# The first layer's modulated input takes its slots half by half

## The chip, the cores and the metric

The kernel runs on one core of a Trainium2 chip. The metric is the device time of one execution in microseconds (us). The core has five engines with an instruction queue each: TensorE (PE in the rows; its weight loads are PEld), VectorE (DVE), ScalarE (ACT), GpSimd (POOL) and SyncE (SP), which here only issues transfers. Each engine works its queue in order; a wait at the head of a queue holds everything behind it.

## The reference, cut to what matters

Two layers of a backbone. Each modulates a normalized input, multiplies it by one wide matrix, runs four branches on slices of the product, and merges them. 128 context tokens and 512 latent tokens go through the same weights with different conditioning vectors (`c_ctx` and `c`).

```python
def trunk_layer(x, cond, p, latent, k_ctx, v_ctx):
    mod = jax.nn.silu(cond) @ p['w_ada'] + p['b_ada']
    shift, scale, gate = jnp.split(mod, 3, axis=-1)
    h = rms_norm(x, p['norm_g']) * (1.0 + scale) + shift
    y, k, v = parallel_mixer(h, p, latent, k_ctx, v_ctx)
    return x + gate * y, k, v
```

`h` of the first layer is what the change is about. Inside `parallel_mixer`, `u = h @ p['w_in']` feeds, among others, a long convolution (Hyena) whose filters are made by a small network, brought into the frequency domain, and multiplied with the transformed input.

## The kernel before

**Numbers and tiles.** All 640 tokens (128 context, 512 latent) are processed together; a projection makes 128 channels at a time, in two pieces of 320 tokens. A product in 32 bits is made of three: the weight and the activation are each split into a rounded part and a rest (`whi`, `wlo`, and `Act.hi`, `Act.lo`), and `proj` adds hi*hi, hi*lo and lo*hi. One piece is 16 matmuls with `whi` and 8 with `wlo`, 24 in all. `split(hi, lo, src)` casts on ScalarE and subtracts on VectorE: that subtraction reads two tiles in SBUF.

**Slots.** SBUF is mostly 13 large slots (`NSLOT`), handed out by `slot()` in the order in which they came free. In the first microseconds they hold the conditioning rows (`s_cond`), the small parameters (`s_prm`), the input of the filter network (`s_hid`), the residual stream in two halves of the channels (`xs[0]`, `xs[1]`: sl_120 and sl_121 in the rows), two filter slots, the tables, and four of the eight chunks of the first layer's modulation matrix `w_ada` (sl_175, sl_178, sl_181, sl_184); the other four chunks lie in weight buffers.

**The start.** `ada_first` takes the chunks in the order 0 4 1 5 2 6 3 7. A chunk is 8 matmuls against the conditioning columns `cs` into an `ax` buffer, a copy to a `k` tile on ScalarE, two transposes of that tile (the `ax<-ident,k` rows) and small additions into `mod` on VectorE. Chunks 0 and 4 give the modulation of channel blocks 0 and 1, chunks 1 and 5 of blocks 2 and 3, and so on: `ev_mod[0][k // 2]`.

**The modulated input.** `modulated_first` (line 758) scales x by the inverse norm, and then, for each half `h` and channel block `c`, transposes the block's tokens to PSUM, applies scale and shift into a `t` tile (latent tokens on ScalarE, context tokens on VectorE), and splits it into `a.h(k)` and `a.l(k)`. Blocks 0 to 3 lie in the first slot of `a.hi` and of `a.lo`, blocks 4 to 7 in the second. The first projection waits for each block by `a.ev[j][k]` (in `proj`). Before the change the function is started by `layers()` only when `new_act(2)` has got all four slots, the two of `hi` first:

```python
            if l == 0:
                a = yield from new_act(2)
                a.ev = [[Event(lm) for _ in range(8)] for _ in range(2)]
                lm.spawn(modulated_first(a, xs, ssq), PN)
```

**What sets the order.** The kernel is written as cooperating threads, run by the planner `Loom` while the program is made: it keeps a modelled time of each engine, and at each `yield` takes the ready thread of the highest priority. PE's order is exactly the order in which the planner let the threads issue; the other engines' orders follow from it and from priorities. So a change in when one thread can go on re-sorts the rest of the program behind it. Two other threads matter here. `Hyena.filters(q)` makes the filters of four channel blocks c, each for two orders q: matmuls `ax<-k,hd`, a product on VectorE, squares on ScalarE, sums on GpSimd, and `spectrum` (the `sc<-sl,sl` and `ax<-sl,sl` rows). `Hyena.run` convolves; when it is done with block 0 it frees slots, and the filter inputs of block 3 are fetched into one of them.

Of the kernel before, what the change touches and what calls it, by code (L numbers as in the profile page):

```python
# [10 lines left out]
F32R = mybir.dt.float32r  # L11
# [220 lines left out]
def hybrid_flow_backbone(ctx: ExitStack, tc: tile.TileContext, i, o):  # L232
# [49 lines left out]
    def slot(dt=F32):  # L282
        yield lambda: 0.0 if free else INF
        return Slot(dt)
# [28 lines left out]
    def split(hi, lo, src, scale=None):  # L313
        if scale is None:
            act.copy(hi, src)
            dve.tensor_tensor(out=lo, in0=src, in1=r32(hi), op=ALU.subtract)
        else:
            act.activation(out=hi, in_=src, func=AF.Copy, scale=scale)
            dve.scalar_tensor_tensor(out=lo, in0=src, scalar=scale, in1=r32(hi),
                                     op0=ALU.mult, op1=ALU.subtract)  # L320
# [53 lines left out]
    def slots(n, dt=F32):  # L374
        r = []
        for _ in range(n):
            r.append((yield from slot(dt)))
        return r

    def new_act(n):  # L380
        hi = yield from slots(n, F32R)
        lo = yield from slots(n, F32R)
        return Act(hi, lo)
# [365 lines left out]
    def rms(ssq):  # L749
        n = ssq.shape[1]  # L750
        v = sm.tile([P, 5], F32, tag="rmsv", name=nm("rmsv"))[:, 0:n]
        rs = sm.tile([P, 5], F32, tag="rmsr", name=nm("rmsr"))[:, 0:n]
        dve.tensor_reduce(out=v, in_=ssq, axis=AX.X, op=ALU.add)
        dve.tensor_scalar(out=v, in0=v, scalar1=1.0 / D, scalar2=EPS, op0=ALU.mult, op1=ALU.add)
        power(rs, v, n)
        return rs

    def modulated_first(a, xs, ssq):

        rs = rms(ssq)  # L760
        for h in range(2):
            xv = xs[h].v(0, 5, 512)
            for t in range(5):
                dve.tensor_scalar(out=xv[:, t, :], in0=xv[:, t, :], scalar1=rs[:, t:t + 1], scalar2=None,
                                  op0=ALU.mult)
        for h in range(2):
            xv = xs[h].v(0, 5, 512)
            yield lm.sync()
            pp = yield from ax.get()
            for c in range(4):  # L770
                pe.transpose(pp[:, 128 * c:128 * c + 128], xv[:, 0, 128 * c:128 * c + 128], ident)
            for c in range(4):
                k = 4 * h + c
                yield ev_mod[0][k // 2]
                ps = yield from mm.get()
                for t in range(4):
                    pe.transpose(ps[:, 128 * t:128 * t + 128], xv[:, 1 + t, 128 * c:128 * c + 128], ident)
                hf = yield from tr.get(T)
                A, S = mods[0][:, 1, k, :], mods[0][:, 0, k, :]
                act.activation(out=hf[:, 128:640], in_=ps, func=AF.Identity, scale=A[:, 1:2], bias=S[:, 1:2])  # L780
                dve.tensor_scalar(out=hf[:, 0:128], in0=pp[:, 128 * c:128 * c + 128], scalar1=A[:, 0:1],
                                  scalar2=S[:, 0:1], op0=ALU.mult, op1=ALU.add)
                mm.put()
                split(a.h(k), a.l(k), hf)
                tr.put()
                for j in range(2):
                    a.ev[j][k].set()
            ax.put()
            xs[h].free()
# [1100 lines left out]
    def layers():  # L1890
# [3 lines left out]
        for l in range(DEPTH):  # L1894
            hy = hys[l]
            if l == 0:
                a = yield from new_act(2)
                a.ev = [[Event(lm) for _ in range(8)] for _ in range(2)]
                lm.spawn(modulated_first(a, xs, ssq), PN)
            hT[0] = a  # L1900
# [77 lines left out]
            if l + 1 < DEPTH:  # L1978
# [3 lines left out]
                a = yield from new_act(2)  # L1982
# [79 lines left out]
    lm.spawn(ada_first(chunks), 3)  # L2062
    lm.spawn(first_sums(*x_first), 4)
    lm.spawn(layers(), 6)
    with tc.manual_schedule(engines={mybir.EngineType.PE}):
        lm.run()
# [94 lines left out]
```

## Time and profile before

| | us |
|---|---|
| median of 3 runs | 2257.85 |
| lowest, highest | 2257.24, 2259.43 |
| the profiled execution | 2260.89 |
| its span (first to last instruction) | 2258.9 |

| engine | busy us | share of the span |
|---|---|---|
| PE | 2191.6 | 97% |
| DVE | 1320.8 | 58% |
| ACT | 1191.5 | 53% |
| POOL | 593.5 | 26% |

The profile is one execution. The busy share says that TensorE is the bound; what it doesn't say is how much of a stretch TensorE ran at its lower clock, which the column of the granted clock shows (1.00 is 2.4 GHz, 0.50 is 1.2 GHz, and a stretch between is a mixture).

### The profile page before, as it was taken

To read this page: it belongs to the slowest core of one execution; us is meant where nothing else is said; L and a number is where in the kernel's file an instruction comes from. 1 tells how busy PE (TensorE), PEld (TensorE's weight loads), DVE (VectorE), ACT (ScalarE), POOL (GpSimd) and SP (SyncE) were. 2 spreads that over 40 slices of the span, in tenths; PEclk is the share of its full clock that TensorE was granted. 3 is DMA by queue.
4 is the path that set the end of the run, shared out by engine and by line. 5 is a ranking of instruction groups with operands and counts; after the bars stand their busy time and mean duration, and the time that the engine had idled before them with its cause. 6 is when DMAs were issued, how large, how long until landed. Compare 5 with 4: busy or idle time off the path is not lost. (4 is left out here: it accounts for less than half of the span.)

```text
span 2258.9 us, 39947 instructions
## 1 busy us (share of the span) xinstructions
PE 2191.6 (97%) x15951; PEld 2141.9 (95%) x15951; DVE 1320.8 (58%) x2736; ACT 1191.5 (53%) x2179; POOL 593.5 (26%) x456
## 2 busy tenths in 40 slices
PE   5998999999999999999999999899999999999999
PEld 3898999999999999999998999899999999999998
DVE  5676686466669965344224768746655898512222
ACT  5554456576664336444446453667766533544441
POOL 2644321111111222564221332111111122222221
PEclk9999999999999999999999999999999999999999
DMA  9476776454658888787899765575555788698985
GB/s 278 113 155 134 157 152 115 91 111 81 106 108 163 150 141 174 156 166 162 150 224 206 140 115 126 130 144 102 93 105 108 144 150 150 121 159 147 172 175 132
DMA packets 510534, 322.31 MB, mean 143 GB/s; under 512 B 13016, under 2 KB 499608, under 8 KB 510093
## 3 DMA queue, kind: packets, MB, share of 16 engines
q0 software_dynamic: 223856, 122.96, 42.9%
q1 hardware_dynamic: 285780, 196.68, 28.8%
q8 instruction: 125, 2.05, 0.4%
q14 instruction: 60, 0.49, 0.1%
q10 hardware_dynamic: 713, 0.14, 0.0%
HBM read 302.26 MB, written 17.47 MB: 142 GB/s over the span
## 5 line engine op out<-in xcount | busy, mean ns | idle before, releaser
L192 PE MATMUL mm<-sl,whi 128*128 128x320 f32 x6304 | 1061.9, 313 | 9.5 <-ACT whi L177 2.9
L192 PEld LDWEIGHTS mm<-sl,whi 128*128 128x128 f32 x6304 | 951.1, 189 | 17.9 <-DVE sl L177 4.7
L192 PE MATMUL mm<-sl,wlo 128*128 128x320 f32 x3152 | 552.2, 311 | 0.5 <-DMA wlo<-in_w_in_dram 0.5
L346 POOL DMA_DIRECT2D wlo<-in_w_in_dram x173 | 264.5, 1529 | 891.6 <-ACT wlo L177 648.1
L192 PEld LDWEIGHTS mm<-sl,wlo 128*128 128x128 f32 x3152 | 482.4, 188 | 1.7 <-DMA wlo<-in_w_in_dram 0.7
L177 ACT CAST whi<-raw 128x1024 fp32r<-128x1024 f32 (+2 forms) x272 | 255.3, 939 | 400.9 <-PE mm L192 379.6
L177 ACT ACTIVATE wlo<-whi 128x1024 fp32r<-128x1024 f32 (+2 forms) x269 | 254.9, 948 | 29.5 <-PE mm L192 26.1
L177 DVE SCALAR_TENSOR_TENSOR t<-t,mm 128x320 f32<-128x320 f32 x192 | 93.0, 485 | 288.2 <-PE mm L192 239.7
L192 PE MATMUL mm<-whi,sl 128*128 128x256 f32 x1600 | 227.3, 285 | 1.9 <-ACT u L177 1.5
L177 DVE SCALAR_TENSOR_TENSOR sc<-sl,prm,sc 128x640 f32<-128x640 f32 (+14 forms) x232 | 207.4, 894 | 9.5 <-ACT sc L177 4.9
L192 PEld LDWEIGHTS mm<-whi,sl 128*128 128x128 f32 x1600 | 204.6, 189 | 4.2 <-ACT u L177 2.2
L192 PE MATMUL sc<-sl,sl 128*128 128x128 f32 (+1 forms) x1344 | 202.4, 292 | 2.7 <-DVE u L177 1.6
L177 DVE TENSOR_TENSOR h<-ax,h 128x512 fp32r<-128x512 f32 (+1 forms) x200 | 120.8, 604 | 121.8 <-ACT h L177 120.5
L192 PEld LDWEIGHTS sc<-sl,sl 128*128 128x128 f32 x1344 | 178.6, 192 | 4.6 <-DVE u L177 2.3
L177 ACT ACTIVATE t<-mm 128x320 f32<-128x320 f32 x208 | 89.7, 432 | 118.5 <-PE mm L192 116.3
L177 ACT ACTIVATE u<-u,nb 128x640 f32<-128x640 f32 x128 | 106.3, 831 | 64.9 <-DVE u L177 64.7
L177 DVE TENSOR_SCALAR_CACHE_REDUCE u<-sc,rq 128x640 f32<-128x640 f32 x128 | 112.7, 881 | 43.8 <-PE sc L192 42.6
L177 ACT CAST h<-ax 128x512 fp32r<-128x512 f32 (+1 forms) x200 | 102.8, 515 | 58.9 <-PE ax L201 57.4
L192 PE MATMUL mm<-wlo,sl 128*128 128x256 f32 x800 | 127.5, 282 | 3.1 <-DMA wlo<-in_w_in_dram 3.1
L201 PE MATMUL ax<-ident,u 128*128 128x128 f32 x752 | 119.8, 274 | 5.9 <-ACT u L177 3.2
L192 PE MATMUL ax<-h,sl 128*128 128x256 f32 (+1 forms) x656 | 121.1, 296 | 1.2 <-DVE h L177 0.6
L192 PEld LDWEIGHTS mm<-wlo,sl 128*128 128x128 f32 x800 | 109.1, 189 | 3.3 <-DMA wlo<-in_w_in_dram 3.3
(203 smaller groups left out, 2224.6 us busy)
## 6 DMA issues: line engine op xcount, KB each, us to landing
raw<-in_w_in_dram SPq DMA_DIRECT2D x176, 512.0 KB
wlo<-in_w_in_dram POOLq DMA_DIRECT2D x173, 512.0 KB, 6.6
wlo<-in_w_ada_dram SPq DMA_DIRECT2D x19, 512.0 KB
whi<-in_w_ada_dram SPq DMA_DIRECT2D x19, 512.0 KB
raw<-in_wo_attn_dram SPq DMA_DIRECT2D x16, 512.0 KB
wlo<-in_wo_attn_dram POOLq DMA_DIRECT2D x16, 512.0 KB, 6.3
raw<-in_w_out_dram SPq DMA_DIRECT2D x16, 512.0 KB
wlo<-in_w_out_dram POOLq DMA_DIRECT2D x16, 512.0 KB, 6.1
```

The source lines that it names most:

```text
L177: r = f(*args, **kw)
L192: r = self.real.matmul(out, lhsT, rhs, **kw)
L201: r = self.real.transpose(out, in_, ident)
L346: nc.gpsimd.dma_start(out=lo[:, 0:w].rearrange("p (k c) -> p k c", k=kk), in_=src.bitcast(F32R), accum_op=ALU.add)
```

## The change

`modulated_first` is now started at once with an empty `Act`, and takes its slots itself: at the start of each half one for `hi` and one for `lo`. The first half needs two free slots instead of four, and the scaling of x needs none. `layers()` no longer waits there and goes on to take the slots of the Hyena branch.

```diff
--- before.py
+++ after.py
@@ -765,6 +765,8 @@
                                   op0=ALU.mult)
         for h in range(2):
             xv = xs[h].v(0, 5, 512)
+            for part in (a.hi, a.lo):
+                part.append((yield from slot(F32R)))
             yield lm.sync()
             pp = yield from ax.get()
             for c in range(4):
@@ -1894,7 +1896,7 @@
         for l in range(DEPTH):
             hy = hys[l]
             if l == 0:
-                a = yield from new_act(2)
+                a = Act([], [])
                 a.ev = [[Event(lm) for _ in range(8)] for _ in range(2)]
                 lm.spawn(modulated_first(a, xs, ssq), PN)
```

No instruction is added or removed on TensorE; the order changes. Three places show how.

PE in the first 45 us, before: the chunks' matmuls (`<-wlo,cs`, `<-whi,cs`, `<-sl,cs`), their transposes (`<-ident,k`) and the filters' matmuls (`<-k,hd`).

```order
L201 MATMUL ax_310<-ident,k_299 128x128 x2
L192 MATMUL ax_315<-wlo_164,cs 32x256 x4
L192 MATMUL ax_315<-whi_165,cs 32x256 x4
L201 MATMUL ax_339<-ident,k_324 128x128 x2
L192 MATMUL ax_346<-sl_175,cs 32x256 x8
L192 MATMUL ax_357<-k_326,hd_191 128x256 x4
L192 MATMUL ax_366<-k_326,hd_191 128x256 x4
L201 MATMUL ax_372<-ident,k_355 128x128 x2
L192 MATMUL ax_393<-sl_178,cs 32x256 x8
L192 MATMUL ax_404<-k_334,hd_191 128x256 x4
```

The same place after, with the transposes of the first half (`<-ident,sl_120`).

```order
L201 MATMUL ax_325<-ident,k_299 128x128 x2
L192 MATMUL ax_330<-wlo_164,cs 32x256 x4
L192 MATMUL ax_330<-whi_165,cs 32x256 x4
L201 MATMUL ax_341<-ident,sl_120 128x128 x4
L201 MATMUL mm_346<-ident,sl_120 128x128 x4
L201 MATMUL mm_356<-ident,sl_120 128x128 x4
L201 MATMUL ax_361<-ident,k_339 128x128 x2
L192 MATMUL ax_368<-sl_175,cs 32x256 x8
L201 MATMUL mm_384<-ident,sl_120 128x128 x4
L201 MATMUL mm_394<-ident,sl_120 128x128 x4
L201 MATMUL ax_399<-ident,k_377 128x128 x2
L192 MATMUL ax_404<-sl_178,cs 32x256 x8
```

All five groups of transposes of the first half now stand beside chunks 5 to 2, ahead of chunk 6 (sl_178); before, they stood around chunk 7. The filters' matmuls that stood between the chunks have moved behind chunk 3.

PE where the first projection begins (mm_533), before: the second half of x is sl_121.

```order
L192 MATMUL ax_541<-k_334,hd_191 128x256 x2
L192 MATMUL mm_533<-sl_301,whi_528 128x320
L192 MATMUL mm_533<-sl_309,whi_528 128x320
L201 MATMUL ax_554<-ident,sl_121 128x128 x4
L201 MATMUL mm_559<-ident,sl_121 128x128 x4
L201 MATMUL mm_569<-ident,sl_121 128x128 x4
```

The same place after; the first projection is mm_572, and chunk 7 is sl_184.

```order
L192 MATMUL ax_468<-sl_184,cs 32x256 x8
L201 MATMUL ax_479<-ident,sl_121 128x128 x4
L201 MATMUL mm_484<-ident,sl_121 128x128 x4
L201 MATMUL ax_489<-ident,k_477 128x128 x2
L201 MATMUL mm_501<-ident,sl_121 128x128 x4
L192 MATMUL ax_511<-k_422,hd_191 128x256 x4
L201 MATMUL mm_517<-ident,sl_121 128x128 x4
L201 MATMUL mm_527<-ident,sl_121 128x128 x4
L192 MATMUL ax_540<-k_422,hd_191 128x256 x2
L192 MATMUL ax_551<-k_430,hd_191 128x256 x4
L192 MATMUL mm_572<-sl_316,whi_567 128x320
```

The second half's transposes now follow chunk 7 directly and are all ahead of the first projection; before, they cut into it.

DVE at about 190 to 202 us, before: the spectral product of block 1 (`sl_171`, `sl_427`, `wx`), and the sum of a modulation chunk of the second layer (`mod_1646<-ax_1939`).

```order
L177 TENSOR_TENSOR sl_189<-ax_1918,sl_1771 128x512
L177 TENSOR_TENSOR wx_190<-sl_427,sl_171 128x640
L177 TENSOR_TENSOR sl_171<-sl_427,sl_171 128x5x128 x2
L177 TENSOR_TENSOR sl_427<-sl_171,wx_190 128x5x128
L177 TENSOR_TENSOR sl_427<-sl_171,sl_499 128x5x128
L177 TENSOR_REDUCE mod_1646<-ax_1939 128x4
```

The same place after.

```order
L177 TENSOR_TENSOR sl_189<-ax_1948,sl_1748 128x512
L177 TENSOR_TENSOR sl_324<-wx_190 128x512 x2
L177 TENSOR_REDUCE mod_1627<-ax_1981 128x4
L177 TENSOR_TENSOR wx_190<-sl_324,sl_171 128x640
L177 TENSOR_TENSOR mod_1627<-mod_1627,prm 128x4
L177 MEMSET sl_189 1x128
L177 TENSOR_TENSOR sl_171<-sl_324,sl_171 128x5x128 x2
```

The sum that frees the chunk's `ax` buffer now stands ahead of the five products instead of behind them.

## Rows read from the trace of the kernel before

**Rows 1.** Page, span and part 1: engine, busy us, share, instructions.

```profile
span 2258.9 us, 39947 instructions
PE 2191.6 (97%) x15951; PEld 2141.9 (95%) x15951; DVE 1320.8 (58%) x2736; ACT 1191.5 (53%) x2179; POOL 593.5 (26%) x456
```

**Rows 2.** Timeline of PE, 46 to 91 us: start, us, work [idle before <-releaser].

```profile
46.82 1.09 PE L192 MATMUL ax<-sl,cs 128*32 128x256 f32 x16
47.85 1.53 PE L201 MATMUL mm<-ident,sl 128*128 128x128 f32 x12
...
53.42 0.86 PE L192 MATMUL mm<-sl,whi 128*128 128x320 f32 x4 [2.87 <-ACT whi L177]
...
59.42 0.41 PE L192 MATMUL mm<-sl,whi 128*128 128x320 f32 x1 [0.86 <-DVE sl L177]
...
66.26 0.41 PE L192 MATMUL mm<-sl,whi 128*128 128x320 f32 x1 [1.35 <-DVE sl L177]
...
67.30 0.38 PE L192 MATMUL ax<-ones,sl 128*128 128x1 f32 x2 [0.51 <-POOL sl L177]
...
68.80 1.65 PE L192 MATMUL sc<-sl,sl 128*128 128x128 f32 x6 [0.78 <-POOL sl L177]
...
82.49 0.38 PE L192 MATMUL ax<-ones,k 128*128 128x1 f32 x2 [1.10 <-POOL k L177]
...
90.90 2.53 PE L192 MATMUL mm<-sl,whi 128*128 128x320 f32 x16
```

**Rows 3.** Stretches: from:to, us, busy by engine, then granted clock, DMA share, GB/s.

```profile
50.00:60.00 10.00, 6.25 (x34) 5.54 (x34) 9.89 (x16) 7.07 (x11) 8.87 (x7) 0.83 0.23 57
60.00:80.00 20.00, 17.17 (x109) 16.13 (x108) 13.79 (x34) 10.94 (x24) 13.79 (x13) 0.83 0.46 129
180.00:190.00 10.00, 6.92 (x49) 6.00 (x50) 3.94 (x9) 7.92 (x15) 1.58 (x1) 0.83 0.71 136
200.00:210.00 10.00, 8.03 (x36) 8.03 (x37) 7.81 (x20) 3.00 (x7) 5.43 (x6) 0.66 0.08 29
```

**Rows 4.** Timeline of DVE, 48 to 53 us: the subtractions of the split.

```profile
48.28 0.83 DVE L177 TENSOR_TENSOR sl<-t,sl 128x640 fp32r<-128x640 f32 x1 [0.98 <-ACT sl L177]
...
50.64 4.02 DVE L177 TENSOR_TENSOR sl<-t,sl 128x640 fp32r<-128x640 f32 x2
```

**Rows 5.** Timeline of POOL, 50 to 54 us.

```profile
50.62 1.54 POOL L177 TENSOR_TENSOR sl<-sl 128x640 f32<-128x640 f32 x1 [20.28 <-DVE sl L177]
52.51 1.47 POOL L177 TENSOR_TENSOR k<-k,k 128x512 f32<-128x512 f32 x1 [0.35 <-ACT k L177]
```

**Rows 6.** Timeline of ACT, 47 to 53 us.

```profile
47.52 0.72 ACT L177 CAST sl<-t 128x640 fp32r<-128x640 f32 x1
...
52.32 1.04 ACT L177 CAST whi<-raw 128x1024 fp32r<-128x1024 f32 x1
```

**Rows 7.** Timelines of SP, ACT, DVE and PE: the fetch of block 3.

```profile
175.82 0.57 SPq L324 DMA_DIRECT2D sl<-in_c_decay_dram  x1
...
179.75 1.25 ACT L177 CAST k<-sl 64x256 fp32r<-64x256 f32 x3 [5.79 <-DMA sl<-in_hy_w_dram]
...
181.03 0.48 DVE L177 SCALAR_TENSOR_TENSOR k<-sl,nob,k 66x256 fp32r<-66x256 f32 x1 [4.89 <-ACT k L177]
...
183.09 0.86 PE L201 MATMUL ax<-ident,sl 128*128 128x128 f32 x5 [3.25 <-DVE sl L177]
```

**Rows 8.** Timelines of DVE and PE, 195 to 203 us.

```profile
195.09 1.91 DVE L177 TENSOR_TENSOR wx<-sl,sl 128x640 f32<-128x640 f32 x1
...
201.76 0.16 DVE L177 TENSOR_REDUCE mod<-ax 128x4 f32<-128x16 f32 x1
...
201.97 0.80 PE L192 MATMUL ax<-k,hd 128*128 128x256 f32 x2 [2.75 <-DVE mod L177]
```

**Rows 9.** Waits of PE, whole span: waiter, releaser, us in total, times, longest.

```profile
PE ax L201 <- ACT k L177: 5.1, 3, 3.6
...
PE mm L192 <- DMA wlo<-in_w_in_dram: 3.5, 2, 3.1
```

## The prediction

> **What bounds the kernel now.** I read the page's busy shares first. TensorE is busy 97% of the span, 2191.6 of 2258.9 us [rows 1], and the change adds and removes no TensorE instruction, so it can only move the 67 us in which TensorE idles, and the time in which it works at its lower clock. The timeline of TensorE shows where the change bites: chunk 7, the last of the modulation matrix, is multiplied from 46.82 us and its transposes follow; then comes a broken stretch. Six waits there make 2.87 + 0.86 + 1.35 + 0.51 + 0.78 + 1.10 = 7.5 us [rows 2]. The first waits for the rounded weight of the first projection (a cast on ScalarE at 52.32, queued behind the modulated input's casts [rows 6]), the next two for subtractions that make `a.l`, the last three for GpSimd sums of the filters.
>
> The granted clock is the second thing to see. It is 0.83 in 50 to 60 and in 60 to 80 us [rows 3]. With two levels, 1.00 (2.4 GHz) and 0.50 (1.2 GHz), that is 10 x 0.17 / 0.5 = 3.4 us and 20 x 0.17 / 0.5 = 6.8 us at the lower one, on which half is lost: 1.7 + 3.4 = 5.1 us. Each such stretch follows waits. So the start loses 7.5 + 5.1 = 12.6 us after chunk 7.
>
> The same pair stands twice more in the first layer. At 183.09 TensorE has waited 3.25 us on a chain that starts with the fetch of the filter inputs of block 3: issued at 175.82, landed for ScalarE's cast at 179.75, then a VectorE step at 181.03, and behind that step the convolution output which TensorE wants [rows 7]. At 201.97 it has waited 2.75 us for a `mod` sum on VectorE that only frees an `ax` buffer [rows 8]. The clock is 0.83 in 180 to 190 and 0.66 in 200 to 210 [rows 3]: 3.4 and 6.8 us at 1.2 GHz, 1.7 and 3.4 us lost. These two places cost 4.95 and 6.15 us.
>
> **The change part by part.** *What does not move.* The order up to chunk 5 is the same, and chunk 7 can't come earlier, since its data are the end of a long row of transfers. So I compare from chunk 7's end, 47.9 us (46.82 + 1.09 [rows 2]), and ask how much of the 12.6 us is still lost behind it. *Work moved past that point.* Three groups of transposes that stood behind chunk 7 (12 in 1.53 us [rows 2]) go ahead of it, eight filter matmuls go behind it; at no more than the 2.53 / 16 = 0.16 us of a wider projection matmul [rows 2] that is 1.3 us. These cancel.
>
> *The start.* All transposes of the second half now follow chunk 7, and its ScalarE and VectorE work with them, while the first half is finished while the chunks still arrive. Three prices decide. (a) The weight cast: it now stands behind two activations instead of four activations, three casts and a square, so I put the first projection at about 52.0 us instead of 53.42. (b) The last subtraction of the second half. VectorE's queue holds from there four subtractions of 0.83 us [rows 4], two weight subtractions of 1024 elements instead of 640 (1.3 us each by that measure) and a filter product of 512 (0.7): 52.0 + 3.3 + 2.6 + 0.7 = 58.6 us if none meets GpSimd. In the rows it does meet it: two subtractions side by side with GpSimd sums took 4.02 us, 1.2 us more each than 0.83 [rows 4, 5]. Three meetings make 62.2 us. TensorE has some 15 projection and 6 filter matmuls to do until then, 3.1 us. So it waits 58.6 - 52.0 - 3.1 = 3.5 us, or 7.1 us; I take the middle, 5.3. (c) GpSimd's sums begin later than before, since the filter matmuls do; their three waits in the rows are 0.51 + 0.78 + 1.10 = 2.4 us, and I take 2.0 (1.7 to 2.4), as there is now a whole piece of projection to hide the later ones. The clock falls after such waits: one stretch of 3.4 us (1.7 lost) to one of 6.8 (3.4 lost); I take 2.5. Sum after: 5.3 + 2.0 + 2.5 = 9.8 us, between 6.9 and 12.9. Against 12.6 that is **-2.8 us** (-5.7 to +0.3).
>
> On (b) a rule bears that speaks against the change. The row shows a subtraction of two SBUF tiles stretched beside a GpSimd sum, by 1.2 us. The Trainium skill (SBUF — State Buffer, section "SBUF: two separate sides") says that VectorE, when it reads two SBUF inputs, and GpSimd contend for one pair of ports as "an exclusive lock, not a bandwidth split", so that whoever comes second waits the whole instruction out. By that rule a meeting could cost all of a GpSimd sum, 1.5 us here [rows 5], and three of them would put (b) at 8.0 instead of 7.1 us; the trace agrees as far as it goes, with 1.2. The rule also says that the first half gains, because GpSimd is idle from 30.3 to 50.62 us, where its four subtractions now stand.
>
> *The fetch of block 3.* It still hangs on VectorE's end of block 0. Between the inverse transform of block 0 and the first TensorE instruction that needs the fetch the order has 72 projection matmuls and one transform before, 56 and three transforms after, about 0.7 us more; and what waits first is now the filter's matmul, which needs only the step at 181.03 and not the four VectorE steps behind it, about 1.6 us earlier (183.09 - 181.5). 3.25 - 2.3 = 1.0 us left, and half of the 1.7 us of clock: **-3.1 us**, between -4.95 (all gone) and +1.0 (VectorE comes a microsecond later instead, as the transform before it stands closer).
>
> *The buffer at 201.97.* The sum that frees the buffer stands behind five products before, and ahead of them after, as the third place of the order shows. In the rows the products took from 195.09 to 201.76 [rows 8]. So this wait goes. What is late next is the filter product behind them: VectorE reaches it 12 to 15 us after the block's transform, TensorE after 14. So 0 to 1 us of wait comes back, with up to all of the clock: between -6.15 and 0, **-4.0 us** taken.
>
> *The rest.* The order differs in most of the first layer and again in the middle of the second. Both hold single waits of 3.1 and 3.6 us [rows 9] that a new order may remove or double, and the dense stretches from 84 to 180 us, without any wait over 0.25 us now, can only get some. I take **+1.5 us**, half of one such wait; bounds -4 and +6.
>
> Sum: -2.8 - 3.1 - 4.0 + 1.5 = -8.4 us. The profiled execution took 2260.9 us, 2.0 more than its span; after the change 2252.5. The median of the runs is 3.0 us lower than the profiled execution, and from it the sum gives 2257.85 - 8.4 = 2249.45, **2249.5 us**.
>
> **Rivals.** *The gain stops at the start.* The two later waits are ends of chains that the new order has too: block 3 is still fetched into a slot that the convolution frees, and one VectorE queue still carries products, filter sums and convolution. If another late piece takes each one's place, -2.8 us remains: 2255 us, too close to tell from no change. For: both places read almost alike in the two orders. Against: the `mod` sum is plainly ahead of the products now.
>
> *GpSimd holds the second half up (slower).* Place: VectorE's queue from 52 to 65 us. If not three but five two-input steps meet GpSimd sums, at 1.2 us each, the last subtraction ends at 64.6 and TensorE waits 9.5 us; the sums, met by as many subtractions of 0.83 us, come 4 us later and TensorE waits 6 us on them; both drops of the clock stay with 3.4 us. 9.5 + 6.0 + 3.4 = 18.9 instead of 12.6 us is +6.3; with the later waits as they were, 2264 us. It decides from about four meetings. For: GpSimd is busy 8.87 of 10 us in 50 to 60 [rows 3]. Against: its sums now start behind a square that ScalarE reaches only at about 54 us, when half the subtractions are done.
>
> *Everything goes well.* Both later waits go with their clock, the start gains 5: -15 us, 2243 us.
>
> *A new wait in the second layer.* The waits there of 3.6 us [rows 9] come twice: +6 on the sum, 2255.5 us.
>
> *That the change doesn't do what it says* I rule out: the order shows the first half's transposes ahead of chunk 6, and their inputs, x and chunks 0, 4, 1 and 5, are there.
>
> **How the numbers follow.** A difference of 0.2%, 4.5 us, is about what a measurement of this kernel can tell from no change. Forecast (2245 to 2253): 0.50. Gain at the start alone: 0.24, of which some 0.06 lies beyond 0.2%. GpSimd: 0.09. All well: 0.09. New wait: 0.08. Faster by over 0.2% (below 2253.3): 0.48 + 0.06 + 0.09 = 0.63; slower: 0.09; the same: 0.28. The forecast's own range is 2245 to 2253. The range for 8 in 10 takes in most of the first rival and the new wait, and half of the case where all goes well: 2243 to 2258.
>
> **What would show it.** Right: transposes of sl_120 before 42 us; four subtractions of the first half at 0.83 us each with GpSimd idle; the first projection at about 52 us; one wait of 3 to 7 us before its last hi*lo matmul; no wait of over 1 us on a `mod` sum near 200 us, and a granted clock near 1.00 in 200 to 210. Wrong: subtractions of the second half over 2 us each with TensorE waiting beyond 62 us; a wait of 3 us or more after the fetch of block 3; new waits in 84 to 180 us; or a second layer whose waits differ by more than 4 us in sum.

## The result, and the profile after

The changed kernel takes 2246.92 us (median of 5 runs, 2244.46 to 2252.46); the kernel before takes 2259.32 in the same comparison (5 runs). The ratio is 0.9949, with a 95% interval of 0.9938 to 0.9960: 9 to 14 us faster. The forecast was 2249.5 in a range of 2243 to 2258, a gain of 8.4 us.

The page of the changed kernel, span and part 1, answers to [rows 1]: as many instructions on each engine, a span 13.9 us shorter, TensorE 7.3 us less busy.

```profile
span 2245.0 us, 39973 instructions
PE 2184.3 (97%) x15951; PEld 2139.7 (95%) x15951; DVE 1329.1 (59%) x2736; ACT 1190.0 (53%) x2179; POOL 587.1 (26%) x456
```

The timeline of TensorE after, 33 to 61 us and the later waits up to 210 us (start, us, work, idle before and releaser), answers to [rows 2]:

```profile
33.70 1.11 PE L201 MATMUL ax<-ident,sl 128*128 128x128 f32 x4
...
45.38 1.75 PE L192 MATMUL ax<-sl,cs 128*32 128x256 f32 x16
...
50.74 0.75 PE L192 MATMUL mm<-sl,whi 128*128 128x320 f32 x4
...
53.86 0.80 PE L192 MATMUL ax<-k,hd 128*128 128x256 f32 x2 [1.90 <-DVE t L177]
...
57.90 0.42 PE L192 MATMUL mm<-sl,whi 128*128 128x320 f32 x1 [0.49 <-DVE sl L177]
...
60.15 0.38 PE L192 MATMUL ax<-ones,sl 128*128 128x1 f32 x2 [1.12 <-POOL sl L177]
...
109.46 0.71 PE L192 MATMUL ax<-sl,sl 128*128 128x128 f32 x4 [1.12 <-DVE fv L177]
...
153.06 1.41 PE L192 MATMUL mm<-sl,wlo 128*128 128x320 f32 x4 [2.73 <-DMA wlo<-in_w_in_dram]
```

The first half's transposes stand at 33.70 us, the first projection begins at 50.74 instead of 53.42, and what follows it waits 1.90 + 0.49 + 1.12 us. Then nothing waits 1 us or more until 109. The waits of 3.25 us at 183.09 and of 2.75 us at 201.97 are gone. In their place stand new ones at 109.46 and 153.06, in a stretch that was dense before.

Stretches of the two kernels, before first (from:to, us, busy and count on PE, PEld, DVE, ACT, POOL, then granted clock, DMA share, GB/s):

```profile
50.00:100.00 50.00, 42.32 (x287) 39.53 (x287) 38.34 (x78) 29.80 (x57) 34.50 (x28) 0.90 0.34 96
100.00:180.00 80.00, 79.60 (x626) 75.77 (x625) 54.77 (x118) 37.23 (x70) 38.59 (x30) 1.00 0.74 157
180.00:210.00 30.00, 24.17 (x151) 23.05 (x152) 20.40 (x39) 15.02 (x30) 13.62 (x11) 0.83 0.56 116
```

and the changed kernel:

```profile
50.00:100.00 50.00, 46.49 (x335) 45.16 (x333) 31.05 (x77) 29.64 (x59) 31.90 (x29) 0.93 0.58 136
100.00:180.00 80.00, 75.63 (x564) 72.06 (x563) 61.15 (x113) 35.24 (x68) 36.39 (x29) 0.94 0.61 134
180.00:210.00 30.00, 29.75 (x238) 28.01 (x237) 23.57 (x49) 17.45 (x36) 18.47 (x18) 1.00 0.58 123
```

What TensorE loses in a stretch is its idle time plus its busy time times (1 - granted clock). From 50 to 100 us it loses 3.5 + 3.2 instead of 7.7 + 4.8 us (clock losses summed over slices of 1 us, here and below). From 180 to 210 it loses 0.2 instead of 10.6. But from 100 to 180 it loses 9.3 instead of 0.4. VectorE is busy 6.4 us more in that stretch: the convolution's work has moved forward, and TensorE, which is ahead, meets its end there. Not all of the 9.3 us is the order's: another execution of the same order (e12 below) loses 3.3 us there.

The table sums this for the pair, and for the other orders that the experiments below ran. "before" and "after" in a name say which start the kernel has; 14.5 and 13.5 are the planner's number changed in the experiments (14.0 in the pair).

| lost by TensorE, us | before | after | before 14.5 | after 14.5 | before 13.5 | after 13.5 | four slots at once |
|---|---|---|---|---|---|---|---|
| 50 to 100 | 12.5 | 6.7 | 11.5 | 7.9 | 12.0 | 8.0 | 8.4 |
| 100 to 180 | 0.4 | 9.3 | 4.8 | 3.9 | 0.0 | 9.0 | 3.5 |
| 180 to 210 | 10.6 | 0.2 | 3.7 | 0.5 | 5.4 | 0.0 | 15.8 |
| 210 to 1300 | 18.9 | 20.1 | 34.4 | 19.9 | 26.4 | 22.5 | 37.0 |
| 1300 to the end | 21.1 | 17.4 | 20.6 | 18.9 | 19.6 | 22.6 | 17.7 |
| median of the runs | 2259.3 | 2246.9 | 2268.4 | 2245.6 | 2261.2 | 2255.5 | 2280.8 |

In the pair these rows make -9.8 us, and TensorE's idle time in the first 50 us (19.8 before, 19.3 after) -0.5: together -10.3 of the 13.9 us between the two spans. The granted clock of the first 50 us is left out, since the column cannot be read there (last section). The other 3.6 us are in no wait and in no low clock that the column shows; they come up again below.

### The profile page after: what moved, and what is told of

Read it like the earlier page. It is cut to its first block, busy times and chain, and to the rows that moved or that the text cites. A ratio compares the mean times of both kernels' runs of the same rounds, so it can differ in the third digit from the quotient of the medians.

```text
span 2245.0 us, 39973 instructions
## 1 busy us (share of the span) xinstructions
PE 2184.3 (97%) x15951; PEld 2139.7 (95%) x15951; DVE 1329.1 (59%) x2736; ACT 1190.0 (53%) x2179; POOL 587.1 (26%) x456
```

## Experiments

Each was timed beside the kernel before; times are medians, ratios are to the kernel before with a 95% interval.

**e1: the fetch of block 3 alone.** In the kernel before, the weights and the bias of block 3's first filter are fetched while block 2's are; TensorE's order stays, row for row.

```diff
+                if (l, c, q) == (0, 2, 0):
+                    self.w3 = op_.tile([P, 256], F32, tag="o", name="w3")
...
+                        sp.dma_start(out=v[r], in_=src)
-                raw = s.v(f0 + T, 256)[0:66]
+                raw = self.w3[0:66] if (l, c, q) == (0, 3, 0) else s.v(f0 + T, 256)[0:66]
```

> The kernel before, with one step changed: the weights and the bias of block 3's first filter are fetched some 100 us earlier into a spare tile, so that only its decay table still waits for the slot. TensorE's order is unchanged. Theory (the wait at 183.09 us is the end of a chain of its own, fetch, cast, VectorE step, and goes when the chain is shortened): the wait of 3.25 us and the low clock behind it (1.7 us lost) go, -3.5 to -5 us. Rival (another end of the same chain takes its place: VectorE's queue, or the decay table, is late next): under 1.5 us gained, and a wait of 2 us or more within 6 us of the same place.

2254.59 us, ratio 0.9980 (0.9968 to 0.9991): -4.5 us. No wait is left at 183; the `mod` wait comes 6 us sooner and as long as in [rows 8]:

```profile
195.69 0.51 PE L192 MATMUL ax<-k,hd 128*128 128x256 f32 x2 [2.80 <-DVE mod L177]
```

The theory holds: the fetch was the end of a chain of its own, and was worth its wait with its clock, 3.25 + 1.7 us, within the error.

**e2: the buffer at 201.97 alone.** In the kernel before, the sum of that one modulation chunk gets a higher priority on VectorE.

```diff
-            with tc.high_priority(offset=HA):
+            with tc.high_priority(offset=WAHEAD if (l, j) == (1, 1) else HA):
                 dve.tensor_reduce(out=m, ...
```

> The kernel before, with one step changed: the sum of the modulation chunk that frees the buffer at 201.97 us gets a higher priority on VectorE and stands behind one product of the block instead of behind all five. TensorE's order is unchanged. Theory (that sum alone holds TensorE): the sum ends near 197 us, the wait of 2.75 us goes and with it the low clock of 200 to 210 us (3.4 us lost), -4 to -6.2 us. Rival (the filter product behind it is late anyway): the wait moves on to that product, 2 us or more stay, and the clock falls as before; less than 2 us gained.

2261.15 us, ratio 1.0007 (0.9996 to 1.0018): no gain. Yet the wait went: from 50 to 210 us this kernel loses 6 us less than before. The timeline of TensorE shows where it went, 20 us on:

```profile
225.51 2.50 PE L192 MATMUL mm<-sl,wlo 128*128 128x320 f32 x8 [3.23 <-DMA wlo<-in_w_in_dram]
```

The timelines of ACT and of GpSimd in the same kernel say what the transfer of this `wlo` had waited for:

```profile
207.65 1.06 ACT L177 ACTIVATE wlo<-whi 128x1024 fp32r<-128x1024 f32 x1
...
206.24 3.54 POOL L177 TENSOR_TENSOR sl<-sl 128x640 f32<-128x640 f32 x3 [4.03 <-DVE sl L177]
209.75 1.86 POOL L177 TENSOR_TENSOR k<-k,k 128x512 f32<-128x512 f32 x1
...
213.32 2.01 POOL L177 TENSOR_TENSOR sl<-sl 128x640 f32<-128x640 f32 x1
...
215.76 1.98 POOL L177 TENSOR_TENSOR sl<-sl 128x640 f32<-128x640 f32 x1
217.69 1.57 POOL L346 DMA_DIRECT2D wlo<-in_w_in_dram  x1
```

ScalarE has its part ready at 208.7. The transfer is issued by GpSimd, whose queue is in order, and six filter sums stand ahead of it until 217.7. It lands 7.8 us later, and TensorE, 5 us earlier than before, is there first. So neither theory nor rival as written: the next late thing was not the filter product but a weight.

**e3: both steps.** The two edits together, in the kernel before.

> The kernel before with both steps: block 3's first weights fetched early, and the sum ahead. TensorE's order is unchanged, the start is that of before. If each wait is an end of its own the gains add: -8 to -11 us, 2248 to 2251 us, as fast as the changed kernel or nearly, without its start. If the gain of the changed kernel comes from its start (the rival), these two together give under 4 us.

2256.87 us, ratio 0.9988 (0.9979 to 0.9996): -2.7 us. From 180 to 210 us it loses 0.2 us, as the changed kernel does, and then 3.33 us at 220.60 for the same `wlo`. Taking both later waits out of the order of before gives a quarter of the changed kernel's gain. Here the rival came nearer, though not for its reason.

**e9: the weight of e2 on VectorE.** The rest of this one weight is subtracted on VectorE, as the kernel does in its first microseconds, instead of by GpSimd's accumulating transfer. (Run after e8; told here since it ends the chain of e2.)

```diff
+            if pooled[0] and count[0] == 334:
+                lm.clk["act"] += (w * act.per + act.fixed) / 1e3
+                nc.vector.tensor_tensor(out=lo[:, 0:w], in0=rv, in1=r32(hi[:, 0:w]), op=ALU.subtract)
-            if pooled[0]:
+            elif pooled[0]:
```

> The kernel of the earlier sum (e2_sum), with one more step changed: of the one weight for which TensorE waits 3.23 us at 225.51 us there, the rest is now subtracted on VectorE, as the kernel does it in its first microseconds, instead of by an accumulating transfer that GpSimd issues. TensorE's order is unchanged. Theory (the gain of the earlier sum was given back because that transfer, ready to go at 208.7 us, stood until 217.7 behind filter sums on GpSimd's queue): the wait at 225 goes with the low clock behind it, and the gain of e2_sum appears: 4 to 6 us faster than before. Rival (another chain, VectorE's queue or the next weight, is late by the same 3 us there): a wait of 2 us or more within 25 us of it stays, and the time is that of e2_sum within 2 us.

2255.92 us, ratio 0.9983 (0.9971 to 0.9994): -3.8 us to before, -5.4 to e2 by ratios. The wait at 225 is gone, and the longest from 190 to 240 us is 0.98. The theory holds: the gain of e2 had been given back at GpSimd's queue. From 210 to 260 us the profile loses 1.0 us where that of e2 lost 6.4. As a whole this one execution (2260.49, among the slowest of its 12) is no faster than before: it loses 15.4 us from 700 to 1300, where e2's lost 8.5. So the gain is read from the medians.

**e4: started at once, but with four slots.** One part of the change alone.

```diff
-            for part in (a.hi, a.lo):
+            for part in (a.hi, a.hi, a.lo, a.lo)[:4 - 4 * h]:
                 part.append((yield from slot(F32R)))
```

> One part of the change alone: the function is started at once, but takes all four slots before its first half, as before. If the halves matter (theory), its first transposes stand behind chunk 2 (TensorE's third chunk from the end) as before, the first projection begins within 1.5 us of before's 53.42, and the first 100 us lose as much as before in waits and low clock (12 us from 48 us on, within 2). If starting at once matters (rival), the start is as in the changed kernel: first projection at about 51 us, 6 to 8 us lost. What the rest of the order makes of it is open by 5 us either way.

2280.8 us, ratio 1.0098 (1.0083 to 1.0113): 22 us slower. The timeline of TensorE, its first transposes, its first projection, the second half's first transposes, and the two later places:

```profile
42.18 0.66 PE L201 MATMUL ax<-ident,sl 128*128 128x128 f32 x4
...
50.94 0.86 PE L192 MATMUL mm<-sl,whi 128*128 128x320 f32 x4 [1.71 <-ACT whi L177]
...
54.75 1.11 PE L201 MATMUL ax<-ident,sl 128*128 128x128 f32 x4 [0.95 <-DVE sl L177]
...
187.53 1.34 PE L201 MATMUL ax<-ident,sl 128*128 128x128 f32 x5 [5.81 <-DVE sl L177]
...
209.57 1.08 PE L192 MATMUL ax<-whi,cs 128*32 128x256 f32 x8 [7.55 <-DVE sl L177]
```

Neither side is right alone. The second half still cuts into the projection, as before; but the transposes come one chunk earlier than before (42.18 for 45.58), the first projection 2.5 us earlier, and 50 to 100 us loses 8.4 us, nearer to the changed kernel's 6.7 than to 12.5. So a good part of the start's gain comes with starting at once alone. Whether it is the scaling, which no longer stands behind the slots, or `layers()`, which goes on, this run does not separate. The loss comes later: 15.8 us from 180 to 210, at the fetch of block 3 again and ahead of a modulation chunk, and 37 us from 210 to 1300. The same start, almost, with a 34 us slower kernel behind it.

**e5 to e8: other orders behind the two starts.** One number of the planner, the distance of the later modulation chunks, is changed in both kernels. TensorE's order is the pair's up to 110 us or more and is sorted anew behind that.

```diff
-ASTEP = 14.0
+ASTEP = 14.5     (e5 before, e6 after; 13.5: e7 before, e8 after)
```

> The kernel before, with one number of the planner changed: the later modulation chunks are 14.5 us of its time apart instead of 14.0. The work and the order of the first 90 us are those of before; the rest of the first layer and part of the second is sorted anew. Theory (the start is worth 4 to 5 us, what the rest of the order adds or takes is chance): this kernel lies anywhere from 6 us faster to 12 us slower than before, with waits of 2 to 6 us at other places of 100 to 600 us. Rival (before's places at 183 and 202 us belong to its start): both waits are there again at the same size within 1 us, and the time is before's within 3 us.

2268.36 us, ratio 1.0037 (1.0023 to 1.0051).

> The changed kernel with the same number changed from 14.0 to 14.5; the order up to about 100 us is that of the changed kernel. Theory (only the start's 4 to 5 us are the change's own): the difference to the kernel before with 14.5 is not the 12 us of the pair with 14.0, but something from -12 to +6 with -5 as its middle; the waits at block 3's fetch and before the filter matmul near 200 us may be back. Rival (the earlier start takes those two waits away by itself): both stay away, and it is 8 to 14 us faster than before with 14.5.

2245.64 us, ratio 0.9933 (0.9918 to 0.9948).

> As the kernel before with 14.5, with 13.5 instead: a second draw of the order behind the same start. Theory: again anywhere from 6 us faster to 12 us slower than before, not the same as with 14.5. Rival: before's time within 3 us and its two waits.

2261.23 us, ratio 1.0003 (0.9993 to 1.0013).

> The changed kernel with 13.5: a second draw behind the changed start. Theory: the difference to before with 13.5 lies anywhere from -12 to +6 us, -5 in the middle, and the four differences (14.0, 14.5, 13.5 and the mean of them) scatter by more than 5 us. In the first 100 us it loses 4 to 5 us less to waits and low clock than before with 13.5. Rival: 8 to 14 us faster than before with 13.5, both waits away.

2255.48 us, ratio 0.9985 (0.9976 to 0.9995).

By the medians the change is worth 12.4, 22.7 and 5.8 us with 14.0, 14.5 and 13.5. The table above takes them apart:
- *The start* is a gain each time, 5.8, 3.6 and 4.0 us from 50 to 100. Up to 100 us the three pairs have one order, so these are three measurements of one gain. Over all profiles here but that of e4, the seven with before's start lose 11.5 to 12.5 us in this stretch, the six with the changed start 6.7 to 8.0: 4.6 us between the means. This is the change's own.
- *The places near 183 and 202.* My theory, that they come and go by chance, falls: all three orders with the old start lose 3.7 to 10.6 us from 180 to 210, all three with the new one 0 to 0.5. The rival is right about the place, but not about the worth. From 100 to 180 the new start loses 3.9 to 9.3 us, the old one 0 to 4.8. From 100 to 210 together it is 11.0, 8.5 and 5.4 us with the old start, 9.5, 4.4 and 9.0 with the new: 8.3 and 7.6 on average. VectorE is busier from 100 to 180 in all three (61, 65 and 63 us against 55, 51 and 57). So some of the waiting did not go, it moved forward. How much is open: three more executions of the changed order on TensorE (e10, e11, e12) lose only 3.8, 3.3 and 3.3 us from 100 to 180, so that some 6 of the pair's 9.3 us are that one execution's. With e12 in its place the three new starts lose 5.6 us on average from 100 to 210, not 7.6.
- *The rest* is what scatters: 18.9 to 37.0 us from 210 to 1300 over the seven columns. Of the 22.7 us with 14.5, 14.5 lie there.

The longest wait from 45 to 600 us of the order with 13.5 and the old start, for comparison; it is again near 200 us, on another tile:

```profile
194.76 0.75 PE L192 MATMUL ax<-k,hd 128*128 128x256 f32 x4 [3.70 <-DVE sl L177]
```

**e10: the new wait at 153.06 taken away.** In the changed kernel, the step of e9 for the weight that is late there (`count[0] == 243`).

> The changed kernel, with the same step for the weight for which TensorE waits 2.73 us at 153.06 us; its transfer there took 11.2 us to land beside those of a modulation chunk and of a weight. TensorE's order is unchanged. Theory A (each wait is an end of its own): the wait of 2.7 us and 3.4 us of lost clock go, 4 to 6 us faster than the changed kernel, 2241 to 2243 us. Theory B (between 100 and 210 us TensorE runs as fast as VectorE's chain of convolution lets it; a wait taken away there is met again at the next end): a wait of 2 to 4 us shows at block 3's fetch (near 180) or at the filter matmul near 198, and the time is that of the changed kernel within 2 us.

2247.41 us, ratio 0.9946 (0.9932 to 0.9959): the changed kernel's time. The wait went and a shorter one came 3 us later:

```profile
156.39 1.44 PE L192 MATMUL mm<-sl,whi 128*128 128x320 f32 x8 [1.71 <-DVE sl L177]
```

From 100 to 180 us this execution loses 3.8 us instead of 9.3, and no wait shows near 180 or 198, so theory B has the wrong place. But the time is what B said, and theory A, a gain of 4 to 6, falls. The profiles of e11 and e12 (below) show a third reading. They have TensorE's order of the changed kernel without this step, and the same matmuls wait less there:

```profile
152.07 0.82 PE L192 MATMUL mm<-sl,wlo 128*128 128x320 f32 x4 [1.42 <-DMA wlo<-in_w_in_dram]
...
152.55 0.83 PE L192 MATMUL mm<-sl,wlo 128*128 128x320 f32 x4 [0.94 <-DMA wlo<-in_w_in_dram]
```

The first line is e11's, the second e12's. The transfer landed after 9.8 and 9.4 us instead of 11.2, no low clock followed, and 100 to 180 us loses 3.3 us in both. So, as far as three profiles can tell, most of what e10 was to save was the loss of one execution, and little of it stands in the median. In the profiled execution of e10 the 5.5 us are used up elsewhere: it idles 2.7 us more before 50 us, 2.0 of them since chunk 7 ends later (49.14 against 47.14), and loses 4.9 us more between 210 and 1300.

**e11: the sum put back.** In the changed kernel, the sum that frees the buffer loses its priority and stands behind the five products, as before.

```diff
-            with tc.high_priority(offset=HA):
+            with tc.high_priority(offset=0 if (l, j) == (1, 1) else HA):
                 dve.tensor_reduce(out=m, ...
```

> The changed kernel, with one step of its order undone: the sum that frees the buffer stands behind the five products again, as in the kernel before. TensorE's order is unchanged. If this place of the queue is what made the wait at 201.97 us (prediction, buffer term): the sum moves from 193.7 to about 201 us, TensorE waits 2 to 5 us for it, the clock falls, and the kernel is 3 to 7 us slower than the changed one, 2250 to 2254 us. If the wait went because TensorE arrives later or has other work there (rival): no wait over 1 us, and the changed kernel's time within 1.5 us.

2250.12 us, ratio 0.9965 (0.9954 to 0.9976): 3.2 us slower than the changed kernel. Timelines of VectorE and of TensorE:

```profile
190.51 2.96 DVE L177 TENSOR_TENSOR wx<-sl,sl 128x640 f32<-128x640 f32 x1
...
197.93 0.17 DVE L177 TENSOR_REDUCE mod<-ax 128x4 f32<-128x16 f32 x1
...
198.15 0.80 PE L192 MATMUL ax<-k,hd 128*128 128x256 f32 x2 [3.81 <-DVE mod L177]
```

The wait of [rows 8] is back, 3.81 instead of 2.75 us, ahead of the same kind of filter matmul. This place of VectorE's queue made it, and the changed order is what removed it. The 3.2 us are little beside the two intervals; the wait, which comes back at its place, is the firmer sign.

**e12: the halves without the early start.** The function is started when the first half's two slots are there.

```diff
-                a = Act([], [])
+                a = yield from new_act(1)
...
-            for part in (a.hi, a.lo):
+            for part in (a.hi, a.lo)[:2 * h]:
```

> One part of the change alone: the halves take their slots one by one, but the function is started only when the first half's two slots are there, as before with four. By the order of the instructions this is the changed kernel again, row for row on all five engines; only other slots hold the data. Theory (the halves are the change, the earlier start and the thread that goes on are not): the changed kernel's time within 2 us, 2245 to 2249, and its waits at the same places. Rival (where the tiles lie in SBUF matters, or the time of one order varies by more than the runs so far show): over 3 us away from the changed kernel.

2247.42 us, ratio 0.9934 (0.9919 to 0.9950): the changed kernel's time. The order of all five engines is that of the changed kernel, so that the early start itself, and that `layers()` goes on, add nothing once the halves need two slots each. The profiled execution took 2252.73, at the top of its runs (2241.90 to 2252.73): from 210 to 1300 us it lost 9.7 us to low clock where the profile of the changed kernel lost 2.9, with the same instructions in the same order. From 100 to 210 it lost 3.5 us, where the profile of the changed kernel lost 9.5 and that of the kernel before 11.0.

None of these is faster than the changed kernel by more than the intervals allow; the lowest ratio is that with 14.5 (0.9933 against 0.9949).

## Why the prediction was right, and where it was not

**The start** (forecast -2.8, between -5.7 and +0.3; found -5.8 in the pair, beyond the bound by 0.1, -3.6 and -4.0 in the other two orders, -4.6 between the means of all profiles). The mechanism was right. (a) The first projection came at 50.74, not 52.0. Of the 2.7 us since before's 53.42 some 0.8 are chunk 7, which ended at 47.14 instead of 47.92; its end lies between 47.0 and 47.9 in the profiles of before's order and between 47.1 and 49.1 in those of the changed one, so that is no part of the gain. From chunk 7's end, as the forecast counts, the projection came after 3.6 us (3.6 in e10 and e11 too, 4.6 in e12); forecast were 4.1, and in all five profiles of before's order it is 5.5. (b) is the step that was mis-sized. It gave 5.3 us to the wait for the last subtraction of the second half; that wait is 0.49 us. I had counted three meetings with GpSimd that VectorE pays for; there was one. Timelines of VectorE and of GpSimd after, answering to [rows 4, 5]:

```profile
50.80 1.22 DVE L177 TENSOR_TENSOR wlo<-raw,whi 128x1024 fp32r<-128x1024 f32 x1
51.93 1.55 DVE L177 TENSOR_TENSOR sl<-t,sl 128x640 fp32r<-128x640 f32 x2
53.40 0.41 DVE L177 TENSOR_SCALAR t<-ax,mod 128x128 f32<-128x128 f32 x1
53.73 1.57 DVE L177 TENSOR_TENSOR sl<-t,sl 128x640 fp32r<-128x640 f32 x1
...
57.04 0.81 DVE L177 TENSOR_TENSOR sl<-t,sl 128x640 fp32r<-128x640 f32 x1
...
53.10 1.51 POOL L177 TENSOR_TENSOR k<-k,k 128x512 f32<-128x512 f32 x1 [22.85 <-ACT k L177]
54.69 3.48 POOL L177 TENSOR_TENSOR k<-k 128x256 f32<-128x256 f32 x2
...
64.94 0.76 POOL L177 TENSOR_TENSOR k<-k 128x256 f32<-128x256 f32 x1
...
66.05 0.48 POOL L177 TENSOR_TENSOR k<-k 128x128 f32<-128x128 f32 x1
```

The first two subtractions run through at their usual 0.8 us each, to 53.48; the second was under way when GpSimd began at 53.10. The third, at 53.73, takes 1.57 us, and the last 0.81. GpSimd pays instead: two sums that take 0.76 + 0.48 us alone take 3.48 here. The larger wait, 1.90 us at 53.86, was in none of my steps: a filter matmul waits for the `ax` buffer with the transposed context tokens, which the scaling into `t` at 53.40 frees, and this stands behind a weight's subtraction (50.80) and two of the tokens'. (c), 2.0 us forecast, was 1.12; the clock, 2.5, was 3.2. Together 6.7 us for 9.8, with the largest wait at a place that I had not named.

**The four subtractions of the first half** ran at 0.8 us each (1.56 for two, twice, from 37.99 and 40.85) with GpSimd idle from 30.3 to 53.1, as forecast.

**The fetch** (forecast -3.1, all gone -4.95). The wait is gone. After, in the timelines of SP, ScalarE, VectorE and TensorE, answering to [rows 7]:

```profile
173.88 0.57 SPq L324 DMA_DIRECT2D sl<-in_c_decay_dram  x1
...
177.50 1.25 ACT L177 CAST k<-sl 64x256 fp32r<-64x256 f32 x3 [1.61 <-DMA sl<-in_hy_w_dram]
...
178.79 0.48 DVE L177 SCALAR_TENSOR_TENSOR k<-sl,nob,k 66x256 fp32r<-66x256 f32 x1 [1.05 <-ACT k L177]
...
180.69 1.45 PE L192 MATMUL ax<-k,hd 128*128 128x256 f32 x10
```

The fetch is issued 1.9 us earlier, the step on VectorE ends at 179.3, and TensorE, which in this execution has waited at 109 and 153, comes for it at 180.69. e1 prices the wait in the old order at 4.5 us.

**The buffer** (forecast -4.0, between -6.15 and 0). Right in place and reason: the sum ends at 193.9 instead of 201.9, ahead of the products, and e11 brings wait and 3.2 us back. That was the price in this order; in the old order (e2) the same wait was worth nothing until a weight's transfer was moved too (e9).

**The rest** (forecast +1.5, between -4 and +6) is the step whose reason failed, and its size came out by luck. With the start at -5.8 and fetch and buffer at -10.4 (10.6 to 0.2 us, for -7.1 forecast), +2.3 us of the spans' -13.9 are left for it. I had put it at half of one wait in the second layer. What it holds is +8.9 us from 100 to 180, +1.2 from 210 to 1300, -3.7 behind 1300 (in the second layer; before, its wait of 2.38 us at 1447 on a `u` tile is gone after), -0.5 before 50 us, and -3.6 in no wait and no low clock. These happen to cancel.

I had written that 84 to 180 us could only get waits, and had named new waits there as a sign of being wrong; they came. And I had not written that they would be the other side of the two terms above: fetch, buffer and 100 to 180 together went from 11.0 to 9.5 us in the pair, -1.5 for the -7.1 of the two terms, and to 3.5 us in e12, -7.5. The experiments that price the two waits singly, e1 (4.5 us, in the old order) and e11 (3.2, in the new), make 7.7. So as terms of their own they were sized about right; how much of them comes back as new waits differs by 6 us between two executions of one order. The fetch was not put back in the changed kernel, so its worth there is not shown.

The total, 12.4 us for 8.4, is that of one order too. With 14.5 and 13.5 the same change at the same start gave 22.7 and 5.8 us, and 22.7 would lie outside the forecast's range. The range held the result of this order; the working behind it does not reach those of the others.

**The open 3.6 us.** Span less all waits and all low clock behind 50 us is 2174.3 to 2176.4 us in the five profiles with before's order on TensorE (before, e1, e2, e3, e9), and 2171.0 to 2172.9 in the four with the changed order (after, e10, e11, e12). So TensorE's own time for the same instructions is some us shorter in this order. It does not go with the start alone: it is 2171.8 and 2175.7 in the two other orders with the old start (14.5, 13.5), 2172.7 and 2171.7 in those with the new. What in an order does it, the runs do not tell.

**The rivals.** GpSimd did not hold the second half up: it was held up itself. The gain did not stop at the start with 14.0 and 14.5; with 13.5 it did, within the error (5.8 us in all, 4.0 at the start). No new wait made the second layer slower in the pair: behind 1300 us it loses 3.7 us less. What is sure to be the change's own is the start's 4.6 us; for the rest three orders are too few to tell the change from chance.

## What to carry to other kernels

Where a planner sorts a program anew, price the place that the change touches, and take the rest from several orders: here the change gained 3.6 to 5.8 us at its own place in three orders, and the totals were 5.8, 12.4 and 22.7. A wait that goes is worth its length only up to the slack of the next chain (e2: nothing; the same with the next chain moved, e9: 3.8 us), so list for each wait what is late next within its length, transfers and the queue that issues them included. Waits in neighbouring stretches that hang on one engine's backlog can trade with each other, so bound them together as well as singly. And look for a new wait in a second execution of the same order before you explain it or remove it: the one at 153 us was 2.73, 1.42 and 0.94 us long in three profiles.

## What the runs showed of the hardware that was not expected

**An accumulating transfer may take 11 us.** Of the transfers of `wlo` that GpSimd issues, the page after has the median from issue to landing as its last column; the second row is the view of the tile `wlo` from 136 to 160 us:

```profile
wlo<-in_w_in_dram POOLq DMA_DIRECT2D x173, 512.0 KB, 6.5
...
DMA to landing us min/median/max: 6.3/8.7/11.2
```

The 11.2 us one was issued at 141.77, with a modulation chunk's two transfers issued 0.4 us earlier and 0.1 us later, and is what TensorE waits for at 153.06. In e11 and e12 the same transfer took 9.8 and 9.4 us.

**A VectorE step with two SBUF inputs that a GpSimd step holds up ends 0.69 us behind it.** Before, at 195.09 us [rows 8], the product took 1.91 us, beside a GpSimd product that ended at 196.32: it ended at 197.00, 0.68 later. After, the subtraction of 53.73 ended at 55.30, GpSimd's sum at 54.61: 0.69. And the product at 193.89 took 2.96 us where 0.82 is usual, beside a GpSimd product that ended at 196.16: 0.69. Timelines of VectorE and of GpSimd after:

```profile
193.71 0.17 DVE L177 TENSOR_REDUCE mod<-ax 128x4 f32<-128x16 f32 x1
193.89 2.96 DVE L177 TENSOR_TENSOR wx<-sl,sl 128x640 f32<-128x640 f32 x1
...
193.94 2.22 POOL L177 TENSOR_TENSOR sl<-sl,sl 128x640 f32<-128x640 f32 x1
```

The step thus runs whole, or nearly, after the other has ended. By the rule that I weighed in the prediction (the Trainium skill, SBUF — State Buffer, section "SBUF: two separate sides": whoever comes second waits the whole instruction out) that is what should be seen, and these three agree with it better than the 1.2 us that I took; it also lets GpSimd be the one that waits, as at 54.69. What the rule did not give is who comes first, and that decided the term. The recorded starts do not always tell it: in the lines above VectorE's start is recorded 0.05 us ahead of GpSimd's, and yet VectorE was held.

**The column of the granted clock cannot be read before its first change.** Eight matmuls of a chunk against `cs` take 1.08 us between 26 and 31 us in every profile, and 0.64 us a little later. At 25 to 35 us the column reads 1.00 in the profile of the changed kernel and 0.50 in that of e10. Timeline and stretch of the changed kernel, then of e10:

```profile
27.71 1.08 PE L192 MATMUL ax<-whi,cs 128*32 128x256 f32 x8 [0.33 <-DMA whi<-in_w_ada_dram]
...
42.13 0.64 PE L192 MATMUL ax<-sl,cs 128*32 128x256 f32 x8
...
25.00:35.00 10.00, 5.94 (x40) 2.61 (x41) 8.51 (x23) 4.15 (x11) 1.20 (x1) 1.00 1.12 333
...
29.29 1.08 PE L192 MATMUL ax<-whi,cs 128*32 128x256 f32 x8 [0.34 <-DMA whi<-in_w_ada_dram]
...
25.00:35.00 10.00, 6.24 (x41) 2.50 (x42) 8.48 (x22) 4.24 (x11) 1.20 (x1) 0.50 1.06 306
```

So 1.00 there does not mean 2.4 GHz, and losses to low clock are counted from 50 us on in this text.

**The low clock differs between executions of one order.** The granted clock cost 2.9 us from 210 to 1300 us in the profile of the changed kernel and 9.7 in that of e12, which has the same order. A difference of a few us in low clock between two single profiles shows nothing. A wait is a firmer sign where it comes back ahead of the same matmuls at the same length (3.25, 3.10 and 3.20 us for block 3 in before, e2 and e9); the wait at 153 us did not.
